# Attention with fillers: pooling operations at a pace of their own, and filler pieces spread to the 79th of 80 units

## The chip, the core and the metric

The kernel runs on one core of one Trainium2 chip. The metric is the device time of one execution in microseconds (us). Engines: PE (TensorE, matrix products and transposes), ACT (ScalarE), DVE (VectorE), POOL (GpSimd), SP (SyncE, which here only issues DMAs).

## What is computed

A decoder block on x of 2048 tokens by 1024 channels, all in float32, in the reference cut to its core:

```python
h = rmsnorm(x, g_mix_pre) * (1 + scale_m) + shift_m
q, k, v, u = split(h @ w_in, [512, 1024, 1536])      # 8 heads of 64; u has 4 groups of 128
attn = stick_breaking_attention(q, k, v)             # strictly causal
pool = pooling_mixer(u, w_pool, pool_scale)          # trailing mean over 2, 4, 8, 16 tokens, minus u
mix = concat([attn, pool]) @ w_out
x = x + gate_m * rmsnorm(mix, g_mix_post)
h = rmsnorm(x, g_ffn_pre) * (1 + scale_f) + shift_f
x = x + gate_f * rmsnorm((silu(h @ w_gate) * (h @ w_up)) @ w_down, g_ffn_post)
```

In the stick-breaking attention the weight of key s for query t is sigmoid(z_ts) times the product of sigmoid(-z_tj) over s < j < t.

## The kernel before

Products of float32 are made of three matmuls each: every operand is split into a high part (an ACT copy) and a low part (a subtraction on DVE or POOL), and `mm3` (line 68) multiplies high by high, low by high and high by low. `split` (line 58) makes the parts.

The tokens are cut into four blocks of 512 (`tb` 0 to 3). A first stage makes the projections of blocks 0 and 1, all of v, and the tokens (`hth`, `htl`) of blocks 2 and 3, which lie in the buffers `hb` (block 2) and `ha` (block 3).

**The attention** (lines 779 to 1010) works on 80 units (h, tb, sc): a head, a block of queries and a block of keys, from the diagonal (sc = tb) down to sc = 0, ten units a head. Each unit has four steps, so the loop (line 967) counts n from 0 to 319, and seven more (`OFF`) to drain. One step issues, by hand and in this order on PE, ACT, DVE and POOL: `values_step` (weights times values, two matmuls), `weights_step` (the scores z for 128 queries, two or three matmuls, and two sigmoids on ACT), `scan_step` (the running product on DVE for the step before, two copies of one column and the multiplication `w` on POOL), `turn_step` (four transposes of weights from seven steps earlier, split by ACT and DVE), and then the fillers. The scan holds 512 elements; DVE has besides it the low parts `wtl`.

**The fillers** are the projections of q, k and u for token blocks 2 and 3, which fit in between the attention's matmuls. `chunks` lists twelve blocks of 128 columns of w_in: q and k for each pair of heads, and the four pooling groups u, of which u0 and u1 follow k1, and u2 and u3 follow k3. `tasks` has each chunk for block 2 and for block 3; the last two chunks are done for block 2 first, and then for block 3. A task is nine pieces: eight of three matmuls and an empty one. `pieces` (line 436) yields after each. Splitting the chunk's weights is woven into it (ACT and POOL).

What follows a task is put into two lists. `urgent` holds what reads the product from PSUM: `store_qk`, which splits and stores q or k in DRAM, or the `take` of `pool_ops` (line 363), two ACT copies and one or two small ones. `small` holds the rest of `pool_ops`: one, two, three or four additions for u0 to u3 (line 387, on POOL while the attention runs), and one subtraction with the store of the result (lines 395 and 396). `run_small` (line 410) does one thing, urgent ones first; `pieces` calls it once after every product piece. So the pooling's operations come one with each piece. After the last task, `fillers` yields once more for each operation that is left.

The rate is set by `goal` (line 985): 34 pieces (`START`) ahead of the loop, and then so that `taken` reaches `N_PIECES` when the area of the first `END` units is done. A step counts 2.5 in a diagonal unit and 4 in another.

q and k come back from DRAM by `block_loads` (line 783), called at the first step of a diagonal unit: two DMAs each for `qt` (two buffers) and `kt` (six), and one for `vt`. SP's DMAs aren't in an order written by hand.

**The output weights** `wo` take the place of the tokens: once `taken` reaches `HB_FREE`, the buffers of block 2 are given to the first four rows of chunks, and when the fillers have ended, those of block 3 to the last four. `wo_load` (line 904) then issues two DMAs of 512 KB in each step.

**The mixing product** begins at the end of the loop: the row tiles 0 and 4 are loaded, added and split at fixed steps from n = 306 on (`FIRST_LOADS`, `FIRST_ADDS`, `FIRST_SPLITS`), and from n = 320 on each step takes three groups of its matmuls, which read `wo_hb` and then `wo_ha`. The last output `o1` (line 864) takes the buffer `um` of the pooling. The FFN follows after it.

Of the kernel before, what the change touches and what calls it, by code (L numbers as in the profile page):

```python
# [45 lines left out]
def block_kernel(ctx, tc, x, c, w_cond, b_cond, g_mix_pre, g_mix_post, w_in, w_pool,  # L46
# [8 lines left out]
    def raw(ap):  # L55
        return ap.bitcast(F32)

    def split(hi, lo, src, low=nc.vector):

        nc.scalar.copy(hi, src)  # L60
        low.tensor_tensor(lo, src, raw(hi), ALU.subtract)  # L61
# [4 lines left out]
    def mm3(ps, terms, first=True, last=True):  # L66

        n = len(terms)
        for i, ((lh, ll), (rh, rl)) in enumerate(terms):
            nc.tensor.matmul(ps, lh, rh, start=first and i == 0, stop=False)  # L70
            nc.tensor.matmul(ps, lh, rl, start=False, stop=False)  # L71
            nc.tensor.matmul(ps, ll, rh, start=False, stop=last and i == n - 1)  # L72
# [79 lines left out]
    def mm_ps(name, alone=False):  # L152
        turn[0] += 1
        return z_ps(name) if turn[0] % 2 and not alone else mm_only(name)
# [202 lines left out]
    def store_qk(tb, ps, dst, name):  # L357
        pool, tag, bufs = (tokp, "e", 2) if tb < 2 else (wst, "e", 1)
        both = pool.tile([P, 2, TB], F32R, tag=tag, bufs=bufs, name=f"{name}_{tb}")
        split(both[:, 0], both[:, 1], ps)  # L360
        nc.sync.dma_start(dst[tb].rearrange("l p t -> p l t"), raw(both))

    def pool_ops(tb, ps, g):

# [40 lines left out]


    small, urgent = [], []
    attending = False

    def run_small():  # L410
        if urgent:
            urgent.pop(0)()
        elif small:
            op = next(small[0], None)
            if op is None:
                small.pop(0)
                run_small()
            else:
                op()
# [3 lines left out]
    def chunk_load(chunk, th, pair=None):  # L423
        kind, m = chunk
        nm = f"w{kind}{m}_{th}"
        w32 = wst.tile([P, KC, P], F32, tag="w32", name=f"{nm}_32")
        n0 = base[kind] + m * P
        nc.sync.dma_start(w32, rows(w_in)[:, :, n0:n0 + P])
        return (w32, *(pair or (wsp.tile([P, KC, P], F32R, tag="wh", name=f"{nm}_h"),
                                wsp.tile([P, KC, P], F32R, tag="wl", name=f"{nm}_l"))))  # L430
# [5 lines left out]
    def pieces(th, chunks, tasks, loaded):  # L436

        loaded = dict(enumerate(loaded))
        todo = {}
        for n in {n: 0 for n, _ in tasks if n not in loaded}:  # L440
            at = KC * [n for n, _ in tasks].index(n)
            todo.setdefault(at + LOAD_AT[th], []).append((n, None))
            for part in range(4):
                todo.setdefault(at + SPLIT_AT[th][part], []).append((n, part))
        for at in sorted(at for at in todo if at < 0):
            for n, part in todo[at]:
                loaded[n] = chunk_load(chunks[n], th)
        for i, (n, tb) in enumerate(tasks):
            kind, m = chunks[n]
            ps = mm_ps(f"{kind}{m}_{tb}", attending)  # L450
            for k in range(KC):
                if k == 0 and th and todo.get(KC * i, [(0, 0)])[0][1] is None:
                    loaded[todo[KC * i][0][0]] = chunk_load(chunks[todo[KC * i][0][0]], th)
                    todo[KC * i].pop(0)
                w = loaded[n]
                mm3(ps, [((w[1][:, k, :], w[2][:, k, :]), tokens(tb, k))],
                    first=k == 0, last=k == KC - 1)
                for c, part in todo.get(KC * i + k, ()):
                    if part is None:
                        loaded[c] = chunk_load(chunks[c], th)  # L460
                    else:
                        chunk_split(loaded[c], part)
                if k == KC - 1:
                    take_chunk(chunks[n], tb, ps)
                run_small()
                yield
            if th == 1:
                yield
# [28 lines left out]
    def drain_small():  # L497
        while small or urgent:
            run_small()

    def weave(main, sides):
# [7 lines left out]
        for ops, _, _ in sides:  # L509
            for _ in ops:  # L510
                pass

    chunks = [("q", 0), ("k", 0), ("q", 1), ("u", 0), ("k", 1), ("u", 1), ("q", 2), ("u", 2), ("k", 2),
              ("u", 3), ("q", 3), ("k", 3)]
# [268 lines left out]
    def block_loads(h, tb):  # L783
        hp, j = h // 2, h % 2
        r = slice(j * DH, (j + 1) * DH)
        kt = qkp.tile([P, TB], F32R, tag="kt", bufs=6, name=f"kt{h}_{tb}")
        vt = att.tile([P, 4, P], F32R, tag="vt", bufs=6, name=f"vt{h}_{tb}")
        kv[h, tb] = kt, vt
        qt = qkp.tile([P, 2, TB], F32R, tag="qt", name=f"qt{h}_{tb}")
        for l in range(2):  # L790
            half = slice(l * DH, (l + 1) * DH)
            nc.sync.dma_start(raw(qt[half]), qd[hp][tb][:, r, :].rearrange("l d t -> d l t"))
            nc.sync.dma_start(raw(kt[half]), kd[hp][tb][l, r, :])
        nc.sync.dma_start(raw(vt), vd[tb][:, h, :].rearrange("(b p) e -> p b e", p=P))
        return qt
# [73 lines left out]
    def unit_loads(u):  # L869
        h, tb, sc = u  # L870
        if sc == tb:
            qts[h, tb] = block_loads(h, tb)

    chunks = []
    for hp in range(4):
        chunks += [("q", hp), ("k", hp)]
        chunks += [("u", g) for g in {1: (0, 1), 3: (2, 3)}.get(hp, ())]

    def fillers():
        yield from pieces(1, chunks, tasks, [first_filler])  # L880
        while small or urgent:
            run_small()
            yield

    tasks = [(n, tb) for n in range(len(chunks) - 2) for tb in (2, 3)]
    tasks += [(n, tb) for tb in (2, 3) for n in (len(chunks) - 2, len(chunks) - 1)]
    fill = fillers()
    N_PIECES = 9 * 2 * len(chunks) + 10
    units = [(h, tb, sc) for h in range(HEADS) for tb in range(NTB) for sc in range(tb, -1, -1)]
    area = [2.5 if tb == sc else 4.0 for _, tb, sc in units]  # L890
    wo, wo_next = [], 0
    HB_FREE = N_PIECES - 10 - 18 + 1
    END = 78
    START = 34
    for _ in range(START):
        next(fill)
    taken = START
    attending = True
# [3 lines left out]
    steps = [(u, i) for u in units for i in range(4)]  # L902
# [26 lines left out]
    def mix_add(T, m32, l32):  # L929
        nc.gpsimd.tensor_tensor(m32[:, 0:HK], m32[:, 0:HK], l32, ALU.add)  # L930
        return T, m32
# [26 lines left out]
    def mix_pieces(count):  # L958
        while products and count:
            if next(products[0], 0) == 0:  # L960
                products.pop(0)
            else:
                count -= 1
# [3 lines left out]
    for n in range(len(steps) + OFF):  # L967

        late_values = len(waiting) > LAG and waiting[0][0][1] == waiting[0][0][2] and waiting[0][1] == 0
        if len(waiting) > LAG and not late_values:  # L970
            values_step(*waiting.pop(0))
        if n < len(steps):
            u, i = steps[n]
            if i == 0:
                unit_loads(u)
            weights_step(u, i)
            spent += 2.5 if u[1] == u[2] else 4.0
        if len(scans) > 1 or n >= len(steps) and scans:
            scan_step(*scans.pop(0))
        if n >= OFF:  # L980
            u, b = steps[n - OFF]
            waiting.append((u, b, *turn_step(u, b)))
        if late_values:
            values_step(*waiting.pop(0))
        goal = START + (N_PIECES - START) * spent / (4 * sum(area[:END]))
        while fill is not None and taken < goal:
            taken += 1
            if next(fill, 0) == 0:
                fill = None
        for pool, here in ((hb, not wo and taken >= HB_FREE), (ha, len(wo) == 4 and fill is None)):  # L990
            if here:
                hi, lo = (pool.tile([P, 4, D], F32R, tag=tag, name=f"wo_{pool.name}{tag}")
                          for tag in ("hi", "lo"))
                wo.extend((hi[:, k, :], lo[:, k, :]) for k in range(4))
        if wo_next < len(wo):
            wo_load()
        if n in FIRST_LOADS:
            firsts.append(mix_load(SEQUENCE[FIRST_LOADS.index(n)]))
        if n in FIRST_SPLITS:
            products.append(mix_products(*mix_split(*firsts.pop(0))))  # L1000
        if n in FIRST_ADDS:
            firsts[0] = mix_add(*firsts[0])
        if n >= len(steps):
            mix_pieces(PER_STEP)
    for a in waiting:
        values_step(*a)
        mix_pieces(PER_STEP)
    mix_pieces(4 * KC)
    order.close()
    ph1.close()  # L1010

# [95 lines left out]
    steps = []  # L1107
# [432 lines left out]
    steps, ops1_at = halves()  # L1540
# [106 lines left out]
```

## Time and profile before

| | us |
|---|---|
| median of 3 runs (2304.04 to 2306.79) | 2305.58 |
| profiled execution, time | 2306.12 |
| profiled execution, span from first to last instruction | 2304.3 |
| first z of the attention (from the span's start) | 312.3 |
| last z of the attention | 823.9 |
| busy: PE / DVE / ACT / POOL | 2261.8 / 1623.4 / 1162.4 / 1307.4 |

Times in rows of the profile are us from the span's start. A row of busy times in stretches gives the stretch, its length, and for each engine the busy time and the number of instructions; then the granted clock of PE as a share of full speed, the mean busy share of the DMA engines, and GB/s. A row of a timeline gives start, duration, engine, source line, operation, and the tiles out<-in. A row of waits gives who waited for whom: us in total, times, the longest. The ends of PE's matmuls are modelled, so that a gap shorter than some 0.15 us between two starts doesn't show as idle; L60 and L61 are the two lines of `split`, L70 to L72 those of `mm3`.

### The profile page before, as it was taken

Reading aid. Unit: us, or ns where it says so; the run is one execution under the profiler, and the core shown is the slowest. Engines: PE = TensorE matmul, PEld = TensorE weight load, DVE = VectorE, ACT = ScalarE, POOL = GpSimd, SP = SyncE. Lnnn points to the kernel's source line nnn. Section 1 sums busy time; section 2 is a strip of 40 time slices with the busy share of each in tenths; the row PEclk is TensorE's granted clock in tenths of the full one; section 3 lists DMA queues with packets and bytes.
Section 4 is the critical chain, followed back from the end, with each engine's and each line's share of the span. In section 5 each row is a group of like instructions: output and inputs, shape, how many; then the busy total and the mean of one; then the engine's idle time right before and its main releaser. Section 6 shows DMA issues by size and latency. Waiting matters only on the chain.

```text
span 2304.3 us, 33463 instructions
## 1 busy us (share of the span) xinstructions
PE 2261.8 (98%) x10733; PEld 1859.8 (81%) x10733; DVE 1623.4 (70%) x2222; ACT 1162.4 (50%) x2408; POOL 1307.4 (57%) x1616
## 2 busy tenths in 40 slices
PE   7999999999999999999999999999999999999997
PEld 4878888888888778887888888888888888888886
DVE  6774559999999967667656565787766566555566
ACT  4324559899998854444323322455533323234453
POOL 3552347787778945555777778331476665641004
PEclk9999999999999999999999999999999999999999
DMA  8885763433435536674555555876753333328663
GB/s 292 279 283 192 283 184 114 121 96 104 122 104 164 164 98 218 218 228 160 166 165 158 164 161 170 278 241 215 252 183 111 109 110 96 114 87 304 205 190 128
DMA packets 312971, 405.17 MB, mean 176 GB/s; under 512 B 19862, under 2 KB 180186, under 8 KB 312668
## 3 DMA queue, kind: packets, MB, share of 16 engines
q1 hardware_dynamic: 308476, 400.68, 54.5%
q10 hardware_dynamic: 4320, 2.36, 0.4%
q8 instruction: 85, 1.39, 0.3%
q14 instruction: 90, 0.74, 0.1%
HBM read 274.51 MB, written 128.45 MB: 175 GB/s over the span
## 4 chain that ended last, share of the span: by engine, by line
PE 89%; DVE 4%; DMA 2%; ACT 2%; POOL 2%; issue 1%; SPq 0%; POOLq 0%; DVEq 0%; ACTq 0%
PE wt L845 4%; PE t_g L70 3%; PE t_g L71 3%; PE t_u L71 3%; PE t_u L70 3%; PE t_u L72 3%; PE t_g L72 3%; PE dn0p L71 3%; PE dn0p L70 3%; PE dn0p L72 3%; PE dn1p L70 3%; PE dn1p L71 3%; PE dn1p L72 3%; PE b_u L71 3%; PE b_g L71 3%; PE b_g L70 3%
## 5 line engine op out<-in xcount | busy, mean ns | idle before, releaser
L834 POOL TENSOR_TENSOR w<-sg,pr 128x512 f32<-128x512 f32 (+2 forms) x320 | 306.6, 958 | 41.3 <-DVE pr L828 26.1
L1209 POOL TENSOR_TENSOR s<-s,cu 128x512 f32<-128x512 f32 x88 | 131.4, 1501 | 236.7 <-DVE cu L1208 153.8
L828 DVE TENSOR_TENSOR_SCAN pr<-pr,carry,idle 128x512 f32<-128x512 f32 x192 | 243.7, 1269 | 0.0
L815 ACT ACTIVATE sg<-z 128x512 f32<-128x512 f32 (+2 forms) x320 | 184.5, 577 | 51.3 <-PE z L813 23.3
L61 DVE TENSOR_TENSOR wtl<-wt,wth 128x512 fp32r<-128x512 f32 (+1 forms) x320 | 188.4, 589 | 23.2 <-ACT wth L60 21.9
L60 ACT CAST wth<-wt 128x512 fp32r<-128x512 f32 (+1 forms) x320 | 184.1, 577 | 15.2 <-PE wt L845 15.2
L817 ACT ACTIVATE pr<-z 128x512 f32<-128x512 f32 (+2 forms) x320 | 184.0, 575 | 0.0
L845 PE MATMUL wt<-ident,w 128*128 128x128 f32 x1088 | 174.4, 275 | 3.9 <-POOL pr L825 1.9
L61 DVE TENSOR_TENSOR u_s_l<-u_s,u_s_h 128x512 fp32r<-128x512 f32 x66 | 64.7, 980 | 144.7 <-ACT u_s_h L60 144.7
L845 PEld LDWEIGHTS wt<-ident,w 128*128 128x128 f32 x1088 | 129.4, 141 | 32.1 <-POOL w L834 2.8
L1199 ACT ACTIVATE s<-s 128x512 f32<-128x512 f32 x88 | 55.7, 632 | 185.2 <-DVE s L1198 185.2
L860 PE MATMUL av<-wth,vt 128*128 128x512 f32 (+1 forms) x320 | 128.7, 402 | 0.4 <-ACT o L865 0.4
L61 DVE TENSOR_TENSOR u_a_l<-u,u_a_h 128x512 fp32r<-128x512 f32 x66 | 75.8, 1150 | 69.0 <-ACT u_a_h L60 69.0
L861 PE MATMUL av<-wtl,vt 128*128 128x512 f32 (+1 forms) x320 | 118.8, 371 | 3.4 <-DVE wtl L61 2.9
L810 PE MATMUL z<-kt,qt 128*128 128x512 f32 (+2 forms) x320 | 118.8, 371 | 2.7 <-ACT pr L817 1.8
L71 PE MATMUL dn0p<-w0p_l,g0p_h 128*128 128x512 f32 x308 | 120.7, 392 | 0.0
L70 PE MATMUL dn0p<-w0p_h,g0p_h 128*128 128x512 f32 x308 | 120.5, 391 | 0.0
L72 PE MATMUL dn0p<-w0p_h,g0p_l 128*128 128x512 f32 x308 | 120.3, 391 | 0.0
L811 PE MATMUL z<-kt,qt 128*128 128x512 f32 (+2 forms) x320 | 117.0, 366 | 0.0
L71 PE MATMUL dn1p<-w1p_l,g1p_h 128*128 128x512 f32 x292 | 114.4, 392 | 0.0
L70 PE MATMUL dn1p<-w1p_h,g1p_h 128*128 128x512 f32 x292 | 114.2, 391 | 0.0
L72 PE MATMUL dn1p<-w1p_h,g1p_l 128*128 128x512 f32 x292 | 114.1, 391 | 0.0
(682 smaller groups left out, 7128.4 us busy)
## 6 DMA issues: line engine op xcount, KB each, us to landing
g<-in_w_gate_dram SPq DMA_DIRECT2D x42, 512.0 KB, 5.2
u<-in_w_up_dram SPq DMA_DIRECT2D x42, 512.0 KB, 4.1
wc<-in_w_cond_dram SPq DMA_DIRECT2D x32, 512.0 KB, 6.6
qt<-qd SPq DMA_DIRECT2D x64, 256.0 KB, 4.0
wd<-in_w_down_dram SPq DMA_DIRECT2D x44, 256.0 KB, 3.5
tdt<-wd SPq DMA_DIRECT2D x44, 256.0 KB, 2.0
w0p<-tdt SPq DMA_DIRECT2D x44, 256.0 KB, 3.8
w1p<-tdt SPq DMA_DIRECT2D x44, 256.0 KB, 3.5
```

The lines of the kernel that those rows point to most:

```text
L60: nc.scalar.copy(hi, src)
L61: low.tensor_tensor(lo, src, raw(hi), ALU.subtract)
L70: nc.tensor.matmul(ps, lh, rh, start=first and i == 0, stop=False)
L71: nc.tensor.matmul(ps, lh, rl, start=False, stop=False)
L72: nc.tensor.matmul(ps, ll, rh, start=False, stop=last and i == n - 1)
L815: nc.scalar.activation(sg[:, 0:L], z[:, 0:L], AF.Sigmoid, scale=0.125)
L817: nc.scalar.activation(pr[:, 0:L], z[:, 0:L], AF.Sigmoid, scale=-0.125)
L828: nc.vector.tensor_tensor_scan(pr[:, 0:L][:, ::-1], pr[:, 0:L][:, ::-1], idle[:, 0:L], one if carry is None else carry, ALU.mult, ALU.bypass)
L834: nc.gpsimd.tensor_tensor(w[:, 0:L], sg[:, 0:L], pr[:, 1:L + 1], ALU.mult)
L845: nc.tensor.transpose(wt[:, i * P:(i + 1) * P], wss[u][i][:, b * P:(b + 1) * P], ident)
L860: nc.tensor.matmul(av[:, lo0:], vb, wh[:, lo0:], start=first, stop=False)
L1209: nc.gpsimd.tensor_tensor(s, s, u, ALU.mult)
```

## The change

1. The pooling's operations are no longer tied to the pieces: while the attention runs, a piece does an urgent operation if there is one, and nothing else. The loop does one of `small` in each second step (`POOL_EVERY`).
2. The exception: when the fillers have ended and only the last chunk's operations are left, they wait until n is above 320, behind the last `scan_step`.
3. `N_PIECES` counts one piece instead of ten beyond the tasks, and `HB_FREE` is written anew for it (the same piece of the same task). `END` goes from 78 to 79.
4. The chunk u1 moves from behind k1 and u0 to behind k2.
5. `stored` and the assertion only check the order while the program is built.

```diff
@@ pieces
-                run_small()
+                if not attending:
+                    run_small()
+                elif urgent:
+                    urgent.pop(0)()
                 yield
@@ chunks, fillers, pace
-        chunks += [("u", g) for g in {1: (0, 1), 3: (2, 3)}.get(hp, ())]
+        chunks += [("u", g) for g in {1: (0,), 2: (1,), 3: (2, 3)}.get(hp, ())]
 
     def fillers():
         yield from pieces(1, chunks, tasks, [first_filler])
-        while small or urgent:
-            run_small()
-            yield
+        while urgent:
+            urgent.pop(0)()
...
-    N_PIECES = 9 * 2 * len(chunks) + 10
+    N_PIECES = 9 * 2 * len(chunks) + 1
...
-    HB_FREE = N_PIECES - 10 - 18 + 1
-    END = 78
+    HB_FREE = N_PIECES - 18
+    END = 79
     START = 34
+    POOL_EVERY = 2
@@ the loop over the steps, behind the pieces
+
+        if small and (n > len(steps) if fill is None and len(small) == 1 else n % POOL_EVERY == 0):
+            run_small()
         for pool, here in ((hb, not wo and taken >= HB_FREE), (ha, len(wo) == 4 and fill is None)):
@@ behind the loop
     mix_pieces(4 * KC)
+    drain_small()
     order.close()
```

More of the change, by code (lines that the diff above doesn't have):

```diff
@@ L361, in store_qk @@
         nc.sync.dma_start(dst[tb].rearrange("l p t -> p l t"), raw(both))
+        stored.add((name[0], int(name[1]), tb))
     def pool_ops(tb, ps, g):
@@ L407, in block_kernel @@
     small, urgent = [], []
+    stored = set()
     attending = False
@@ L871, in unit_loads @@
         if sc == tb:
+            assert tb < 2 or {("q", h // 2, tb), ("k", h // 2, tb)} <= stored
             qts[h, tb] = block_loads(h, tb)
```

## The prediction

> **What bounds the kernel now.** I read the engines' busy time first, in five stretches of the attention (345 to 784.9 us) and in its tail (784.9 to 826 us), where no filler matmul is left, and then the chain of waits inside each of the two.
>
> ```profile
> core 0: us, PE busy (x) PEld busy (x) DVE busy (x) ACT busy (x) POOL busy (x), PEclk, DMA share, GB/s
> 345.00:436.40 91.40, 91.28 (x534) 77.32 (x534) 89.78 (x117) 83.02 (x188) 70.33 (x158) 1.00 0.38 108
> 436.40:476.20 39.80, 38.26 (x227) 32.65 (x226) 37.02 (x50) 34.40 (x81) 32.52 (x71) 1.00 0.43 113
> ...
> sum 439.90, PE 436.91 PEld 373.01 DVE 427.71 ACT 397.38 POOL 354.64; mean PE 87.38 PEld 74.60 DVE 85.54 ACT 79.48 POOL 70.93
> ```
> ```profile
> 784.90:798.00 13.10, 11.10 (x60) 7.98 (x59) 12.80 (x15) 12.39 (x28) 11.68 (x24) 1.00 1.02 321
> 798.00:806.40 8.40, 6.40 (x39) 4.97 (x38) 7.03 (x12) 5.72 (x13) 8.08 (x16) 0.94 0.35 104
> 806.40:813.00 6.60, 6.60 (x34) 5.50 (x33) 5.54 (x6) 4.95 (x10) 3.86 (x11) 0.82 0.72 198
> ...
> sum 41.10, PE 36.12 PEld 27.00 DVE 38.37 ACT 36.06 POOL 35.15; mean PE 9.03 PEld 6.75 DVE 9.59 ACT 9.01 POOL 8.79
> ```
> ```profile
> by line: PE wt L845 21.7%; PE z L810 11.7%; PE av L861 11.6%; PE z L811 11.6%; PE av L860 11.5%; PE u L70 3.1%; PE u L71 3.0%; PE u L72 3.0%; PE k L70 2.6%; PE k L71 2.5%; PE k L72 2.5%; PE z L813 1.8%; PE q L70 1.8%; PE q L71 1.8%; PE q L7
> by line: DVE pr L828 51.9%; DVE wtl L61 25.0%; issue 5.9%; DVE ml L61 4.0%; PE wt L845 3.1%; ACT pr L817 2.9%; ACT wth L60 2.4%; PE av L860 2.1%; PE av L861 1.8%; PE z L811 1.6%; PE z L810 1.6%; POOL pr L825 0.3%; POOL w L834 0.2%; ACT sg L
> ```
>
> The first chain row is that of the main stretch, the second that of the tail. In the main stretch TensorE sets the pace and is idle for 3.0 of 439.9 us; but VectorE is idle for only 439.9 - 427.7 = 12.2 us, so a second bound stands 3% below. In the tail the order is turned round: the chain runs over VectorE's scans, VectorE is idle for 41.1 - 38.4 = 2.7 us, TensorE for 5.0 us. Filler work in front of the tail costs time almost one to one; the same work in the tail is nearly free. That is what the change trades on.
>
> **Part 1, the pace of the pieces.** Before, the goal runs from 34 to 226 by the 78th unit, and the last 10 counts hold no matmul. Working out the goal step by step from the code's areas, the last matmul piece (count 215) is issued at step 292 of 320, in unit 73. Afterwards the goal runs to 217 by the 79th unit: piece 205 is the last issued before step 296, where unit 74 begins, and 206 and 208 to 215 follow up to step 311. So nine pieces of three matmuls leave the main stretch for the tail.
>
> ```profile
> 601.45 0.40 PE L70 MATMUL q<-hth,wq_h 128*128 128x512 f32 x1
> 601.68 0.39 PE L71 MATMUL q<-htl,wq_h 128*128 128x512 f32 x1
> 601.91 0.40 PE L72 MATMUL q<-hth,wq_l 128*128 128x512 f32 x1
> ```
>
> Starts lie 0.23 us apart, a piece is 0.69 us, nine are 6.2 us. The gain lies between 0 (VectorE takes over at once) and 6.2 us (TensorE alone decides). VectorE's 12.2 us of idle time are twice that, but afterwards the two engines would lie within 6 us of each other over 434 us, and every small wait of either counts. I take **-4.5 us**, nearer the upper end, because the chain of this stretch names VectorE only in its small shares.
>
> In the tail these 6.2 us meet 5.0 us of TensorE's marked idle time, and more under the modelled ends of its matmuls, while VectorE's work there is unchanged. What VectorE loses in the tail now comes by way of GpSimd:
>
> ```profile
> PE wt L845 <- POOL w L834: 1.9, 3, 0.8
> PE av L861 <- DVE wtl L61: 1.3, 4, 0.7
> PE wt L845 <- POOL pr L825: 1.0, 1, 1.0
> ```
> ```profile
> 789.27 1.06 POOL L387 TENSOR_TENSOR us<-u 128x527 f32<-128x527 f32 x1
> 801.37 1.29 POOL L395 TENSOR_TENSOR um<-us,um 128x512 f32<-128x512 f32 x1
> ```
>
> The last chunk's five pooling operations (1.06 to 1.29 us each) stand here between the weights, GpSimd is busy for 8.08 of 8.40 us, and the transposes wait 2.9 us for it. **Part 2, the pooling's own pace**, takes that apart: the same operations come one in two steps. The third pooling chunk's second half (four operations) now falls on steps 296 to 302, the last chunk's first on step 312, and its other four behind step 320, past the last weights. GpSimd's load in the tail stays about the same up to step 302 and is lower after it, so I take **-1.5 us** of the 2.7 us that VectorE can win (bounds +1 and -2.7).
>
> Those four late operations (some 4.7 us) lie in the mixing product, where TensorE is the bound and GpSimd is nearly idle. What they meet is the split of the second row tile on VectorE:
>
> ```profile
> 825.18 3.21 DVE L61 TENSOR_TENSOR ml<-m,mh 128x512 fp32r<-128x512 f32 x2
> 835.36 1.28 DVE L61 TENSOR_TENSOR ml<-m,mh 128x512 fp32r<-128x512 f32 x2
> ```
>
> The pair that ran beside GpSimd's work took 3.21 us, the pair without it 1.28: up to +1.9 us, hidden under 16 product pieces of 0.69 us of the first tile. I take 0; without that cover it is 1.9 us. The Trainium skill speaks against the change here: "SBUF — State Buffer", section "Who interferes with whom", says that a VectorE instruction with two SBUF inputs and a GpSimd instruction that reads SBUF exclude each other for the whole instruction. The two rows agree with it; by the rule alone, with every late operation in the way, the sum would be up to 4.7 us worse, by the rows it is 0 to 1.9. The last chunk's store moves with them, and SyncE works in order:
>
> ```profile
> 781.16 0.34 SPq L907 DMA_DIRECT2D wo_hahi<-wod  x1
> ...
> 802.68 0.33 SPq L396 DMA_DIRECT2D mtd<-um  x1
> 803.05 0.43 SPq L907 DMA_DIRECT2D wo_halo<-wod  x1
> ...
> 845.64 0.36 SPq L918 DMA_DIRECT2D m<-mtd  x1
> ```
>
> Before, the last load of the output weights' second burst stood behind it, 21.9 us after the first; issued at about 840 us, it has only row loads behind it, the first of which went out at 845.6 us: 0, and at worst a few us of a load that is read later still. Its buffer is the last output copy's too, which comes after the last values and so behind it.
>
> **Part 3, the chunk order.** q2 and k2 come two tasks earlier: the second half of k2 is done at step 155 instead of 177, for a reader at step 184. Against that, the slower pace moves k3's second half from step 234 to 249, for a reader at 264: still some 15 steps.
>
> ```profile
> PE z L810 <- DMA mtd<-o: 0.6, 1, 0.6
> ```
>
> This wait, at the start of unit 46, reads the late k2 and should go; and u0 and u1 no longer follow each other in the stretch from 436.4 us, where TensorE is idle for 1.5 us. Together **-0.6 us** (bounds 0 and -2.1).
>
> **Part 4, the output weights.** They are loaded into the buffers that the fillers' tokens leave: 8 loads of 512 KB when piece 197 has run (step 263 before, 279 after), 8 more after piece 215 (step 292 before, 311 after). The first burst is shown here with the loads of a query block next to it:
>
> ```profile
> 733.06 0.62 SPq L792 DMA_DIRECT2D qt<-qd  x1
> 734.20 0.34 SPq L907 DMA_DIRECT2D wo_hbhi<-wod  x1
> ...
> 737.87 0.45 SPq L907 DMA_DIRECT2D wo_hblo<-wod  x1
> 738.36 0.67 SPq L792 DMA_DIRECT2D qt<-qd  x1
> 759.17 1.28 SPq L792 DMA_DIRECT2D qt<-qd  x2
> ```
> ```profile
> DMA to landing us min/median/max: 7.4/8.7/10.0
> DMA to landing us min/median/max: 3.4/3.9/4.4
> ```
> ```profile
> 758.51 0.39 PE L810 MATMUL z<-kt,qt 128*128 128x512 f32 x1
> 766.50 0.22 PE L810 MATMUL z<-kt,qt 128*128 128x128 f32 x1
> ```
>
> The landings are wo_hblo's and qt's. Before, the burst split a pair of query loads: the second half went out behind all eight, harmlessly, since its unit started 20 us later. At step 279 the same meeting comes with the pair of 759.17 us, and that pair's first reader is the matmul at 766.50 us. Behind nothing it lands in time (759.84 + 4.4 = 764.2). Only the first two of the eight loads stand ahead of it in the code's order (steps 283 and 284); a quarter of the burst's 13.7 us (734.20 to 737.87 + 10.0) ahead of it, 3.4 us, makes it about 1 us late. I put **+1.0 us** (bounds 0 and +11, the last in the slower rival).
>
> The second burst now starts behind step 311 (about 812 us by the old clock) and its first reader is this:
>
> ```profile
> 831.68 0.39 PE L70 MATMUL mix<-wo_hahi,mh 128*128 128x512 f32 x1
> ```
>
> 812 + 13.7 = 826 us: on time, 0.
>
> **The sum**: -4.5 - 1.5 - 0.6 + 1.0 = -5.6 us. The profiled execution took 2306.12 us (span 2304.3) and would take 2300.5; the median of the runs lies 0.54 us lower, so **2300.0 us**, 0.24% faster.
>
> One thing is left out of it. The granted clock in the tail was 0.94 and 0.82 (rows above), which withholds 8.4 x 0.06 + 6.6 x 0.18 = 1.7 us from TensorE. With fillers there it may stay at 1.00; as VectorE leads the chain there, I add nothing. The Trainium skill, "TensorE: Matmul & The Clock Gate", section "HAM oscillation — how this bites in real kernels", has the clock fall after idle gaps above some 3.4 us; the longest wait in the tail is 1.0 us, so by that rule nothing would be withheld, and the trace doesn't agree. By the rule the sum stays -5.6, by the rows it could reach -7.3.
>
> **Rivals.** (1) VectorE is the floor: relieving TensorE moves the idle time across. For it: 97% busy in the main stretch. Against: every chain row there. Main -1, tail -0.5, the rest as above: -1.1 us, 2304.5 us. (2) On the other side: all eight loads of the first burst go out before the second half of the query pair, as they did at 734.20 us. It decides if SyncE's order puts them so; the half then lands at 760.2 + 13.7 + 3.9 = 777.8 us instead of before 766.5, TensorE stands for 11.3 us, VectorE behind it, and a clock cut as in the row of 806.4 us (1.2 us) may follow: -6.6 + 12.5 = +5.9, 2311.5 us. Against: all but two of these loads come later in the code than the pair. (3) The second burst is late: SyncE, working in order, stretched it over 21.9 us before; behind 812 us, and with the 10.0 us of a slow landing, the last of it would come at 844 us, four groups of three matmuls behind the first reader at 831.7 us: some 9 us, +3.4, 2309.0 us. Against: the store that it waited for is moved away. (4) The change doesn't do what it says where the late operations are moved into GpSimd's queue ahead of the last weights: the tail's 1.5 us are lost, 2301.5 us; this is within the forecast's own range.
>
> **How the numbers follow.** Forecast with (4) 0.54, (1) 0.21, (2) 0.17, (3) 0.08. The forecast's own range is 2295.6 (-6.2 - 2.7 - 2.1 + 1.0 from the median) to 2302.5; the whole range reaches up over (1) and (3) to 2308.5, leaving (2) and a few per cent out. About 0.2% (4.6 us) is what a measurement can tell from no change: faster by more than that (below 2301.0) has some six sevenths of the forecast, 0.46; slower (above 2310.2) has (2) but for its cheaper forms, and half of (3), 0.17; within it the rest, 0.37.
>
> **What would show it.** Right: the first z of unit 74 comes 4 to 5 us earlier, VectorE's idle time between 345 us and there falls below 9 us, filler matmuls reach unit 77, and no transpose waits for GpSimd behind 798 us. Wrong: idle TensorE before the z of unit 71 or 73 with a DMA as releaser (rival 2), before a mixing product on wo_ha (3), or unit 74 starting no earlier with VectorE's idle time near zero (1).

## The result and the profile after

| | before | changed | ratio, 95% interval |
|---|---|---|---|
| median of 20 runs each, us | 2304.90 | 2302.16 | 0.9986 (0.998 to 0.9992) |
| span of the profiled execution, us | 2304.3 | 2302.6 | |

The change is faster by 0.14%, some 3.2 us (the medians lie 2.7 us apart); 5.6 us were forecast. Ratios use fast runs alone: one slow execution of e1 (5842 us) and one of the kernel before (2813 us) stay out of them.

The two profiled executions must not be subtracted as they stand: the changed one reaches the first z of the attention 2.4 us later (314.7 against 312.3 us), on code that is the same up to there. Over ten profiles of this study that start lies between 310.3 and 315.9 us, and among the four of e5 to e8, taken on one chip, between 311.4 and 315.9; it varies from run to run. So I measure the attention from its first z to its last one, cut at the first z of units 6, 70 and 74:

| us | before | changed | difference |
|---|---|---|---|
| units 0 to 5 | 32.74 | 31.97 | -0.8 |
| units 6 to 69 | 415.50 | 411.46 | -4.0 |
| units 70 to 73 | 24.33 | 26.43 | +2.1 |
| unit 74 to the last z | 38.98 | 37.86 | -1.1 |
| first to last z | 511.54 | 507.73 | -3.8 |
| last z to the end | 1480.4 | 1480.1 | -0.3 |

These stretches repeat much better: the four kernels that are alike in units 6 to 69 (the changed one, e1, e2 and e5) take 411.5 to 411.6 us there. Units 0 to 5 repeat less well: e4, which is the kernel before up to there, takes 32.39 us, so 0.35 of the -0.8 us is scatter.

The same stretches as rows of busy time (columns as before), first units 6 to 69 and the tail of the kernel before, then all five of the changed kernel:

```profile
345.07:760.57 415.50, 412.89 (x2423) 351.96 (x2422) 404.77 (x525) 376.08 (x856) 334.10 (x732) 1.00 0.42 117
784.90:823.88 38.98, 34.20 (x179) 25.57 (x177) 36.24 (x45) 33.94 (x74) 33.03 (x70) 0.96 0.60 178
```
```profile
314.74:346.71 31.97, 31.08 (x177) 25.64 (x176) 29.00 (x39) 29.08 (x70) 21.78 (x54) 1.00 0.47 133
346.71:758.17 411.46, 408.67 (x2399) 347.20 (x2398) 404.26 (x526) 373.75 (x853) 329.61 (x727) 1.00 0.39 108
758.17:784.61 26.44, 24.22 (x151) 20.93 (x149) 23.34 (x33) 21.35 (x54) 21.79 (x46) 1.00 0.85 251
784.61:822.47 37.86, 36.56 (x205) 29.49 (x204) 36.06 (x45) 34.24 (x75) 32.85 (x72) 1.00 0.52 161
822.47:2302.60 1480.13, 1464.83 (x6495) 1204.12 (x6493) 946.04 (x1300) 574.95 (x1098) 784.05 (x574) 1.00 0.54 176
```

TensorE has 24 matmuls less in units 6 to 69 (its count falls from 2423 to 2399), and the stretch is 4.0 us shorter: 0.17 us for each, of the 0.23 us by which their starts lie apart. VectorE's work there is unchanged (404.8 us before, 404.3 after), so its idle time went from 10.7 to 7.2 us, while TensorE's stayed near 2.7. The chain of waits inside this stretch and inside the tail, of the changed kernel:

```profile
by line: PE wt L850 17.1%; DVE pr L833 15.0%; PE av L866 10.0%; PE z L816 9.3%; PE z L815 9.2%; PE av L865 9.1%; DVE wtl L61 7.5%; PE u L70 2.7%; PE u L71 2.7%; PE u L72 2.6%; PE k L70 2.0%; PE k L71 1.9%; PE k L72 1.9%; PE z L818 1.4%; PE 
by line: PE wt L850 14.0%; DVE pr L833 13.2%; issue 11.6%; PE z L816 8.0%; PE z L815 8.0%; PE av L866 7.2%; PE av L865 6.9%; DVE wtl L61 6.2%; PE u L70 4.3%; PE u L71 4.3%; PE u L72 4.3%; POOL um L396 3.4%; ACT wth L60 2.7%; ACT pr L822 2.6
```

Read them beside the two rows of before: there the main stretch showed TensorE's lines in front, and the tail was VectorE's for three quarters. Now both stretches look alike, with VectorE on the chain for a fifth. Two bounds that lay apart, one in front and one behind, have been brought together, and what is left to gain in this way is small.

In the tail the clock is back. Rows of four stretches of it:

```profile
784.60:797.10 12.50, 12.50 (x72) 10.44 (x71) 11.63 (x15) 12.09 (x26) 10.66 (x24) 1.00 0.54 145
797.10:804.60 7.50, 6.84 (x45) 5.72 (x44) 7.50 (x11) 5.85 (x15) 7.18 (x16) 1.00 0.47 140
804.60:812.10 7.50, 7.50 (x42) 6.24 (x41) 7.10 (x9) 5.94 (x13) 5.46 (x13) 1.00 0.00 1
812.10:822.47 10.37, 9.73 (x51) 7.09 (x50) 9.84 (x13) 10.37 (x25) 9.57 (x23) 1.00 0.88 310
```

Before, 0.94 and 0.82 were granted in two of its rows. Why it came back is taken up behind the experiments.

The loss of 2.1 us sits in unit 70, and a waits row names it. SyncE's issues around it, and the wait:

```profile
756.77 0.62 SPq L797 DMA_DIRECT2D qt<-qd  x1
757.91 0.34 SPq L913 DMA_DIRECT2D wo_hbhi<-wod  x1
758.30 0.42 SPq L913 DMA_DIRECT2D wo_hblo<-wod  x1
758.77 0.62 SPq L797 DMA_DIRECT2D qt<-qd  x1
759.44 0.59 SPq L913 DMA_DIRECT2D wo_hbhi<-wod  x1
```
```profile
PE z L815 <- DMA qt<-qd: 2.0, 1, 2.0
```

The first pair of output weights split the pair of query loads, as in the sum of the prediction. Half a query block behind 1 MB came 2.0 us late.

Behind the last z, the late pooling operations on GpSimd and the split that they run beside, in the changed kernel's timeline:

```profile
832.68 2.52 POOL L388 TENSOR_TENSOR us<-us 128x525 f32<-128x525 f32 x2
835.16 1.74 POOL L936 TENSOR_TENSOR m<-m,l 128x512 f32<-128x512 f32 x1
836.87 1.27 POOL L388 TENSOR_TENSOR us<-us 128x513 f32<-128x513 f32 x1
838.22 1.29 POOL L396 TENSOR_TENSOR um<-us,um 128x512 f32<-128x512 f32 x1
```
```profile
832.96 2.79 DVE L61 TENSOR_TENSOR ml<-m,mh 128x512 fp32r<-128x512 f32 x2
```

The pair of low parts took 2.79 us instead of 1.28, and TensorE did not wait for it: the rest of the kernel is not longer. Nor did a product wait for the second burst of output weights, the prediction's third rival.

### The profile page after: what moved, and what is told of

It is laid out like the page before. It is cut to its first block, busy times and chain, and to the rows that moved or that the text cites. A ratio compares the mean times of both kernels' runs of the same rounds, so it can differ in the third digit from the quotient of the medians.

```text
span 2302.6 us, 33477 instructions
## 1 busy us (share of the span) xinstructions
PE 2260.8 (98%) x10733; PEld 1859.9 (81%) x10733; DVE 1621.4 (70%) x2222; ACT 1161.4 (50%) x2408; POOL 1309.2 (57%) x1616
## 4 chain that ended last, share of the span: by engine, by line
PE 85%; DVE 8%; DMA 2%; issue 2%; POOL 2%; ACT 1%; SPq 0%; DVEq 0%; POOLq 0%; ACTq 0%
PE wt L850 4%; DVE pr L833 4%; PE t_u L71 3%; PE t_u L70 3%; PE t_u L72 3%; PE t_g L70 3%; PE t_g L71 3%; PE t_g L72 3%; PE dn0p L71 3%; PE dn0p L72 3%; PE dn0p L70 3%; PE dn1p L71 3%; PE dn1p L70 3%; PE dn1p L72 3%; PE b_u L71 3%; PE b_g L71 3%
```

## The experiments

Two theories went in. The relief: the gain comes from the matmuls that left the main stretch, and the query collision takes part of it back. Its rival: the gain comes from the pooling's own pace, since GpSimd was the late engine; and behind both stood VectorE as a floor. Ratios are to the kernel before, with 95% intervals. All lengths below are between first z's, as in the table above.

**The burst behind the query block.**

```diff
-    HB_FREE = N_PIECES - 18
+    HB_FREE = N_PIECES - 17
```

> The changed kernel with one edit: the first burst of output weights begins one piece later, so that all of it stands behind the query block of unit 71 in the code. Collision theory: the wait of about 2.0 us of TensorE before the first z of unit 71 goes, unit 70 takes about 6.0 us instead of 8.1, and the kernel gains about 2 us on the changed one (2304.9 before: about 2299.5, ratio 0.9978). Rival (the wait only moves on): the query block of unit 73 is late instead, TensorE waits about 2 us there and the time stays within 0.5 us of the changed kernel's. Rival (VectorE is the floor): unit 70 gets shorter, and units 71 to 74 longer by as much, since VectorE had 2.6 us of idle time in unit 71 to give back.

2298.94 us, ratio 0.9971 (0.996 to 0.9983). SyncE's issues of this kernel, and the stretch of units 6 to 69, 70 to 73 and the tail as rows of busy time:

```profile
752.42 1.29 SPq L797 DMA_DIRECT2D qt<-qd  x2
753.80 0.54 SPq L913 DMA_DIRECT2D wo_hbhi<-wod  x1
...
758.04 0.43 SPq L913 DMA_DIRECT2D wo_hblo<-wod  x1
759.26 1.80 SPq L797 DMA_DIRECT2D qt<-qd  x2
```
```profile
342.20:753.81 411.61, 408.75 (x2399) 347.16 (x2398) 404.27 (x526) 373.76 (x854) 330.31 (x727) 1.00 0.39 108
753.81:777.96 24.15, 23.96 (x150) 20.97 (x149) 23.11 (x33) 21.36 (x54) 21.66 (x46) 1.00 0.85 274
777.96:815.88 37.92, 36.59 (x206) 29.49 (x205) 36.07 (x45) 34.27 (x76) 32.98 (x73) 1.00 0.53 163
```

Both query loads go out together, the wait is gone, and units 70 to 73 take 24.15 us instead of 26.43. Units 6 to 69 and the tail are as in the changed kernel, and the query block of unit 73, issued behind the whole burst (759.26 us), is in time. The stall was not made up for elsewhere. From first to last z it is 505.6 us, 2.1 less than the changed kernel: by the profiles this version beats both, and its median points the same way, though the two intervals overlap.

**The burst wholly in front of it.**

```diff
-    HB_FREE = N_PIECES - 18
+    HB_FREE = N_PIECES - 20
```

> The changed kernel with the first burst of output weights begun two pieces earlier, so that all eight loads stand ahead of the query block of unit 71 in the code. Collision theory, the price of the prediction's second rival: the second half of the query load goes out behind eight loads instead of two, TensorE waits 10 to 12 us before the first z of unit 71, and the kernel is 8 to 10 us slower than the changed one (about 2311, ratio to the kernel before 1.002 to 1.004). If SyncE's order doesn't follow the code's order: no change, 2 us of wait as in the changed kernel.

2312.36 us, ratio 1.0032 (1.002 to 1.0045); the issues and the wait of this kernel:

```profile
753.78 0.62 SPq L797 DMA_DIRECT2D qt<-qd  x1
754.91 0.34 SPq L913 DMA_DIRECT2D wo_hbhi<-wod  x1
...
758.14 0.68 SPq L913 DMA_DIRECT2D wo_hblo<-wod  x1
758.91 4.24 SPq L797 DMA_DIRECT2D qt<-qd  x3
```
```profile
PE z L815 <- DMA qt<-qd: 10.5, 1, 10.5
```

None, two or eight loads of 512 KB ahead make 0, 2.0 and 10.5 us of wait: the price of the collision, and the prediction's second rival as it would have been. With eight ahead, units 70 to 73 take 13.1 us more than in e1, so the wait is not all of it: from 764.2 to 777.8 us the granted clock was 0.50, as that rival had in part allowed for. Three pieces of filler lie between the gain of e1 and this loss.

**The pooling tied to the pieces again.**

```diff
-                if not attending:
-                    run_small()
-                elif urgent:
-                    urgent.pop(0)()
+                run_small()
...
-        if small and (n > len(steps) if fill is None and len(small) == 1 else n % POOL_EVERY == 0):
+        if small and fill is None and (n > len(steps) if len(small) == 1 else n % POOL_EVERY == 0):
```

> The changed kernel, with the pooling's operations tied to the pieces again, one after each, as before; the pace of the pieces, the chunk order and the late last operations stay. Theory of the relief (TensorE is given 27 matmuls less in front of unit 74): units 6 to 70 keep their 411.5 us to within 0.7 (415.5 before), and the time is the changed kernel's or up to 1 us more. Rival (the pooling's own pace makes the gain, since GpSimd was the late engine in the stretches with u chunks): units 20 to 26 go back from 37.1 towards 39.8 us, units 6 to 70 above 413.5, and the kernel loses 2 to 3 us on the changed one.

2307.39 us, ratio 1.0006 (0.9997 to 1.0015), and 512.3 us from first to last z: without the pooling's own pace nothing of the gain is left. Units 6 to 69 take 413.9 us, as the rival has it (above 413.5), but not for the reason it names: units 20 to 25 go from 37.1 to 37.9 us only, units 40 to 45 from 38.6 to 40.2. From unit 71 on 3.0 us are lost, and the smaller query wait (1.1 us instead of 2.0) gives 0.9 back. Waits of TensorE for GpSimd in the attention, of this kernel and, below, of the changed one:

```profile
PE wt L847 <- POOL w L836: 2.5, 3, 1.3
PE wt L847 <- POOL pr L827: 1.9, 1, 1.9
```
```profile
PE wt L850 <- POOL pr L830: 0.6, 1, 0.6
PE wt L850 <- POOL w L839: 0.2, 1, 0.2
```

4.4 us against 0.8: with one operation after each piece GpSimd is late, and with it the weights that TensorE is to transpose. So the rival holds a large part of the truth; what the spread of the pieces gains even so is told behind the experiments.

**The chunk order alone**, in the kernel before.

```diff
-        chunks += [("u", g) for g in {1: (0, 1), 3: (2, 3)}.get(hp, ())]
+        chunks += [("u", g) for g in {1: (0,), 2: (1,), 3: (2, 3)}.get(hp, ())]
```

> The kernel before, with only the chunk u1 moved from behind u0 to behind k2. Theory of the relief: little; units 20 to 26 lose the 1.5 us of TensorE's idle time at most, units 6 to 70 go from 415.5 to about 414.5, and the ratio is about 0.9997. Rival (the two pooling chunks one behind the other made the largest single loss, 39.8 us against 37.1 for units 20 to 26): units 6 to 70 about 413, ratio about 0.999.

2307.27 us, ratio 1.0009 (1.000 to 1.0018): both expectations missed. Units 20 to 25 keep their 39.7 us, so u1 behind u0 was not what made them long, and units 6 to 69 grow to 417.5 us; 1.5 us of that growth are in units 40 to 49, where u1 now lies. Waits of TensorE for GpSimd, 5.3 us against 3.8 before; the two that came in addition, of 0.6 and 0.9 us, stand in units 43 and 46:

```profile
PE wt L845 <- POOL pr L825: 3.4, 4, 1.0
PE wt L845 <- POOL w L834: 1.9, 3, 0.9
```

**The last operations not held back**, in e1.

```diff
-        if small and (n > len(steps) if fill is None and len(small) == 1 else n % POOL_EVERY == 0):
+        if small and n % POOL_EVERY == 0:
```

> The kernel with the first burst behind the query block (e1), but the last chunk's pooling operations run one in two steps from step 312 on, instead of waiting for the last weights. Theory of the prediction (they make GpSimd late in the tail): from the first z of unit 74 to the last z 37.9 us grow by 0.5 to 1.5 us, with transposes waiting for GpSimd, and the time is about 1 us more than e1's. Rival (one operation in two steps is slow enough for GpSimd): this stretch stays within 0.3 us, and nothing is gained by holding them.

2300.96 us, ratio 0.9976 (0.9966 to 0.9985): not told apart from e1. The tail is 37.93 us against 37.90, and first to last z is 505.6 in both. One wait shows just behind the last z:

```profile
PE wt L850 <- POOL w L839: 1.0, 1, 1.0
```

At one operation in two steps GpSimd keeps up, and holding the last ones is worth 1 us at most; the expectation of 0.5 to 1.5 us in the tail was wrong.

**The pieces spread to the 80th unit**, in e1 (`END = 80`).

> e1 with the pieces spread to the end of the 80th unit instead of the 79th. Theory of the relief: six or seven matmuls less in units 6 to 70, 411.6 us go to about 410.4; from there to the last z about the same. The second burst of output weights starts some 6 us later: if it was nearly late, TensorE waits at a mixing product and the gain is given back (time within 1 us of e1's); if it had time, the time is about 1 us less than e1's. VectorE as the floor: units 6 to 70 stay at 411.6.

2300.61 us, ratio 0.9977 (0.9968 to 0.9987). Six matmuls less in units 6 to 69, yet 412.5 us instead of 411.6: not the relief, and more than the floor. Waits of TensorE:

```profile
PE wt L850 <- POOL w L839: 2.3, 4, 0.8
PE av L866 <- DVE wtl L61: 1.9, 6, 0.6
PE mix L71 <- DMA wo_halo<-wod: 0.5, 1, 0.5
```

TensorE waits 2.3 us for GpSimd, against 0.9 in e1; that the slower pace moves the pooling onto other units is a likely reason, not a shown one. The second burst of output weights begins to be late too (0.5 us).

**The pieces spread to the 75th unit**, in e1 (`END = 75`): the pooling's own pace and the new order, at about the pace of before.

> e1 with the pieces spread to the end of the 75th unit, about the pace of the kernel before; pooling's own pace, late last operations and the changed chunk order stay. Theory of the relief: some 25 matmuls more in units 6 to 70, 411.6 us go to about 416.5 (0.2 us each), and the tail from unit 74 gets shorter by 1 us at most, VectorE being its bound; time 3 to 5 us more than e1's. Rival (the pooling's own pace makes the gain): units 6 to 70 about 413, time within 2 us of e1's.

2304.00 us, ratio 0.9996 (0.9987 to 1.0005). Units 6 to 69 take 416.1 us with 21 matmuls more than e1: 0.21 us for each. The tail, now without fillers, takes 36.2 us, 1.7 less: 27 matmuls cost 0.06 us each there. That is more than the 1 us at most that was expected.

**The same with the order of before**, so that beside the kernel before little but the pooling has changed (the pieces keep its pace to within three matmuls in units 6 to 69).

```diff
-        chunks += [("u", g) for g in {1: (0,), 2: (1,), 3: (2, 3)}.get(hp, ())]
+        chunks += [("u", g) for g in {1: (0, 1), 3: (2, 3)}.get(hp, ())]
```

> As e7, with the chunk order of the kernel before (u1 behind u0): the pooling's own pace alone, beside the kernel before. If the order in itself costs about 2 us, as it did alone (units 6 to 70 417.5 us against 415.5), this one lies 1 to 2 us under e7; if that cost came only from the operations tied to the pieces, the two are within 0.5 us. Against the kernel before: theory of the relief units 6 to 70 at 414.5 to 415.5, ratio 0.9990 to 1.0; if the pooling's pace makes the gain, units 6 to 70 at 412 to 413 and ratio 0.998.

2303.28 us, ratio 0.9991 (0.9982 to 1.000). Units 6 to 69 take 416.2 us, as in e7: at the new pace of the pooling the order costs nothing, though the wait at unit 46, for a k load, is there with the order of before (1.0 us) and not in e7. And they are no shorter than before (415.5), and longer than both expectations had them; but the tail is, 36.2 us against 39.0:

```profile
788.81:825.02 36.21, 33.01 (x178) 24.46 (x177) 35.16 (x44) 33.91 (x74) 28.55 (x64) 1.00 0.63 197
```

TensorE's longest wait in it is 0.7 us, all for VectorE, and the granted clock is 1.00 although no filler matmul is there.

So the way from the kernel before to the changed one can be walked in four steps, each one difference of two profiles from first to last z:

| step | us |
|---|---|
| pooling's own pace, last operations late (before to e8) | 511.54 to 509.08: -2.5 |
| chunk order (e8 to e7) | to 509.01: -0.1 |
| pieces to the 79th unit (e7 to e1) | to 505.60: -3.4 |
| burst one piece earlier (e1 to changed) | to 507.73: +2.1 |

Of the first step, 0.35 us is the scatter in units 0 to 5. And the shares hold for this order of steps alone. Going from e4 to e3, the pieces are spread while the pooling stays tied to them: units 6 to 69 become 3.6 us shorter (417.5 to 413.9), but units 70 to 73 become 3.2 us longer, by the query wait and by 1.9 us of waiting for GpSimd in unit 73. From first to last z 512.29 us are left, no less than before the change; from there the pooling's own pace gives 4.6 us.

## Why the prediction was right, and where it was not

The forecast of 2300.0 us was missed by 2.2 us, inside its range of 2295.6 to 2302.5 but near its upper end.

**The pace of the pieces** was right in mechanism and nearly in size: -4.5 us forecast for the main stretch, -4.0 measured there with the term of the order (-0.6) in it. The step that the rival of the VectorE floor took apart is visible: of 0.23 us for a matmul 0.17 came back, and VectorE's idle time in units 6 to 69 went down with the stretch. The signs that were named came out less well. Counted from the first z, unit 74 starts 2.7 us earlier instead of 4 to 5, and VectorE's idle time from 345 us to there is 10.3 us, not below 9; in e1, without the query wait, it is 4.9 us and 8.4 us. Filler matmuls do reach unit 77. Spreading further no longer pays (e6). With the pooling tied to the pieces the spread still takes 3.6 us off units 6 to 69 (e4 to e3), so the relief of TensorE is real by itself; without part 2 it is lost again behind them.

**The tail** came out at -1.1 us for -1.5, but as a difference of two terms that the prediction had not separated: the pooling's pace gives 2.8 us (before to e8), and the fillers take 1.7 us of it (e7 to e1). It was called nearly free to put them there, and they cost 0.06 us a matmul, a quarter of the price in front. Transposes still wait for GpSimd once there, at 803.9 us, for 0.6 us; none was forecast.

**The late operations** behind the last weights were costed at nothing, with up to 1.9 us hidden; 1.5 us appeared on VectorE and were hidden. Holding them back is worth little by itself (e5). By the Trainium skill, "SBUF — State Buffer", section "Who interferes with whom", a VectorE instruction with two SBUF inputs contends with a GpSimd instruction that reads SBUF, by an exclusive lock; the 2.79 us beside GpSimd against 1.28 us alone agree, and the cost stayed under the products.

**The chunk order** is the step that failed: "should go ... together -0.6 us". The 0.6 us wait at unit 46 did go (with the old order it is there again in e8), but units 20 to 25 had not been long because u1 followed u0. Alone the order costs 1.5 us from first to last z (e4), because u1's operations, at one a piece, make TensorE wait 1.5 us longer for GpSimd in units 43 and 46; with the pooling's own pace it costs nothing. Why units 40 to 49 bear them worse than units 20 to 29 is not settled.

**The query collision** was foreseen with its place and order of issue, and mis-sized: +1.0 us in the sum, 2.1 measured, inside the bounds of 0 to 11. The term set a quarter of the burst, 3.4 us, against the 2.3 us by which the second half had been early (764.2 against 766.50 us). The landing itself was delayed about as forecast, by 3.1 us; the half query took from issue to landing, before and in the changed kernel:

```profile
DMA to landing us min/median/max: 4.3/4.3/4.3
```
```profile
DMA to landing us min/median/max: 7.4/7.4/7.4
```

What the term left out is the issue. SyncE issued the two weight loads in between, so that the second half went out 2.00 us behind the first (756.77 and 758.77 us) instead of 0.67 us, another 1.3 us late: 3.1 + 1.3 - 2.4 makes the 2.0 us. The upper end, 11.3 us for eight loads, was measured as 10.5.

**The clock** had been left out, with 1.7 us as the most. It did come back to 1.00, but it did not need the fillers: in e7 and e8 no filler is in the tail, and it is 1.00 there too. In e3 the fillers are there, and it fell where the tail begins. What the falls have in common is the stretch in front of them; here first the kernel before, then e3:

```profile
801.98:805.39 3.41, 1.63 (x9) 1.07 (x9) 3.04 (x5) 1.90 (x4) 3.25 (x8) 1.00 0.47 126
805.39:808.81 3.42, 3.42 (x11) 2.83 (x12) 1.88 (x2) 1.86 (x4) 2.57 (x11) 0.50 1.08 322
```
```profile
783.42:786.83 3.41, 1.49 (x10) 1.13 (x9) 1.68 (x3) 1.88 (x5) 3.33 (x10) 1.00 0.36 112
786.83:790.25 3.42, 3.42 (x13) 2.84 (x12) 2.00 (x3) 1.73 (x4) 2.67 (x8) 0.50 0.78 206
```

Behind 3.4 us in which TensorE was busy for 1.5 to 1.8 us (e4 has 1.76), 0.50 was granted for the next 3.4 us. Those thin stretches come from waits for GpSimd, 0.8 and 1.0 us before and 1.9 us in e3, which the pooling's own pace takes away. How much of the tail's gain is the clock's is not separated. The Trainium skill, "TensorE: Matmul & The Clock Gate", section "HAM oscillation — how this bites in real kernels", has it fall after idle gaps of more than some 3.4 us; the longest wait in the tail of before was 1.0 us, and the trace doesn't agree.

The terms in the order of the prediction, -4.5, -1.5, -0.6 and +1.0, became -4.0 for the first and third together, -1.1 and +2.1; with -0.8 in units 0 to 5, which hadn't been looked at, and -0.3 behind, that is -4.1 in the profiles; by the ratio of the runs it is -3.2. That the sum came so near is in part luck: the 1.1 us won in units 0 to 5 and behind the last z, where nothing was forecast, make up for the 1.1 us by which the collision was undersized. In part they have a reason (three of the 27 matmuls that left the front lay in units 0 to 5), in part they are scatter. The change lies within 0.2% of the kernel before, for which the chance was 0.37; the forecast itself was faster by a little more than that.

## What to carry to other kernels

When two engines are each busy for 97% of a stretch, what moving work of the first away gains comes out of the second's idle time: here a gain of 4.0 us took it from 10.7 to 7.2 us, and a further step gained nothing (e6). Read how much it is before counting the moved work at its full price, and see whether a third engine must be in time for the gain to show (e3). A change of pace also moves every buffer's release: go through what each freed buffer sets off, and what then stands in the same queue. Here the place of two DMAs in a queue took back 2.1 of the 5.9 us that the rest of the change had gained.

## What the hardware showed

That none, two and eight loads of 512 KB in front of a load of 256 KB made 0, 2.0 and 10.5 us of wait where SyncE issues them all. That the granted clock fell to 0.50 for 3.4 us behind 3.4 us in which TensorE was busy for 1.5 to 1.8 us, with no single wait above 1.0 us in two of the three cases (before and e4), and stayed at 1.00 in the tails without such a stretch, with filler matmuls or without. And that the span before the attention varies by 5.6 us over ten profiles of the same code, more than the whole change; a subtraction of two spans would have halved the gain.
